# Plain float32 for the first twelve input products, x split after them, and the S5 parameters' complex product on VectorE

## The chip, the cores and the metric

The kernel runs on one core of a Trainium2 chip. The metric is the device time of one execution in microseconds (us), as the median of several runs. The engines are named as the profile names them: PE is TensorE (PEld its weight loads), DVE is VectorE, ACT is ScalarE, POOL is GpSimd and SP is SyncE, which here only issues DMAs. Each engine works through its instructions in an order that a scheduler fixed when the kernel was built; engines wait for one another by semaphores.

## The reference

One layer of an encoder over 512 tokens of width 1024, in float32:

```
xn   = rmsnorm(x, mix_norm_w)
proj = xn @ w_in            # 1024 -> 512 + 1024 + 1536 + 32 + 1024 + 1024
u_s5, z, xbc, dt_raw, gate_a, gate_b = split(proj)
y_a  = s5_bidirectional(u_s5, ...)         # 32 groups, 64 complex states, scan both ways
glu  = gelu(y_a) @ w_glu;  y_a = glu[:1024] * sigmoid(glu[1024:])
y_b  = ssd_bidirectional(z, xbc, dt_raw, ...)   # convolution over 5 tokens, chunked scan, w_ssd_out
h    = x + (sigmoid(gate_a) * y_a + sigmoid(gate_b) * y_b) @ w_o
h    = h + peer_ffn(rmsnorm(h, ffn_norm_w), ...)  # 16384 experts, 8 heads, 16 picks of each
out  = rmsnorm(h, final_norm_w)
```

The S5 part needs, for every group, products of two complex factors that come from the parameters alone (powers of lambda times the discretised B).

## The kernel before, in words

**Stages.** The first 560 us or so of the execution are the front part: the norm of x, the products with `w_in`, S5, SSD and the gated linear unit. Then come the merge with `w_o`, the routing and the two forms of the expert layer (dense and gathered), to 1963 us.

**Split products.** Every large product is done with its two operands split: `hi` is the operand rounded to float32r by ACT, `lo` is what is left, made by a subtraction on DVE or POOL. `mm3` (lines 147 to 153) then issues three products for each block of 128 inner elements: hi times hi (L151), hi times lo (L152), lo times hi (L153).

**The stream of jobs.** `stream_T` runs over a list of jobs. A job is one weight tile [128, 8, 128] of `w_in` times x in its transposed form ([128, 8, 512]); its output is [128, 512]. `wload` (L136 to L145) brings the tile of the next job while the present one runs: a DMA that SP issues into `w_raw` (three buffers, L140), a cast by ACT into `w_hi` (L143), a subtraction into `w_lo` (L144) on the engine that a table of zeros and ones names (0 DVE, 1 POOL). Then come 24 products into the tile `mm` and an evacuation by ACT. The jobs come in the order u 0 to 3, gate_b 0 to 3, the convolution's B and C tiles 8 to 11, dt (32 columns wide), the convolution's x tiles 0 to 7, and the rest. Of the first twelve jobs the tables give six `w_lo` to DVE and six to POOL.

**x.** `norm_T` (L189 to L199) transposes x with TensorE into the tile `sm`, and for each of 8 blocks ACT writes `xh` (L197) and DVE writes `xl` (L198).

**S5 beside the stream.** `weave` traces the first 22 jobs (`N_IN`) side by side with S5, which has eight parameter groups q. For each q, `s5_params` (L315 on) makes the factors `mpr`, `mpi` by a complex product, `cmul` (L244 to L250), of six operations over 128x512 on POOL:

```
mr, mi, gt = big("mpr"), big("mpi"), big("s5tmpg")
self.cmul(mr, mi, pw(self.pm[0]), pw(self.pm[1]), ch(bbr), ch(bbi), gt, eng=G)
```

and `x0r`, `x0n` by six operations over 128x512 on DVE (L338 to L344). TensorE takes `mpr` and `mpi` by transposes (L374). `s5_data` does the chunk products (L434 to L436) into `sm`. The convolution of a tile takes four operations on DVE (L464) and one at its end (L466). The rest of the list of jobs is woven with SSD.

**Tiles.** `xh` and `xl` are two tiles of [128, 8, 512] under the tags Ah and Al; in the merge `mh` and `ml` take the same places. `col`, a row of 0 to 127, is made by POOL at the start and used by the routing.

Of the kernel before, what the change touches and what calls it, by code (L numbers as in the profile page):

```python
# [10 lines left out]
F32 = mybir.dt.float32  # L11
# [15 lines left out]
P_GLU = (1,)  # L27
# [12 lines left out]
N_IN = 22  # L40
LAST = 2
# [13 lines left out]
# columns of the array of small parameters  # L55
# [9 lines left out]
def weave(*fibers):  # L65
    """Runs (generator, length) pairs side by side, each at its own pace."""
    live = [[g, 0, float(n)] for g, n in fibers]
    while live:
        live.sort(key=lambda f: f[1] / f[2])
        f = live[0]  # L70
        try:
            next(f[0])
            f[1] += 1
        except StopIteration:
            live.remove(f)


def ahead(tc, gen, offset):
    """The steps of gen, traced at a higher priority."""
# [9 lines left out]
class Kernel:  # L89
# [8 lines left out]
    # ---------------------------------------------------------------- constants  # L98
    def consts(self):
# [4 lines left out]
        # half the taps and biases: silu(x) = (tanh(x / 2) + 1) x / 2  # L104
# [4 lines left out]
        col = cp.tile([128, 128], F32, name="col")  # L109
        nc.gpsimd.iota(col, pattern=[[1, 128]], base=0, channel_multiplier=0,  # L110
                       allow_small_or_imprecise_dtypes=True)
# [3 lines left out]
        self.col = col  # L115
# [14 lines left out]

    def pc(self, name, i=None):
        a, b = PAR[name]
        return self.par[:, a:b] if i is None else self.par[:, a + i:a + i + 1]

    # ---------------------------------------------------------------- products
    def wload(self, src, k, m, name="w", lo_eng=None):  # L136
        """A weight tile [128, k, m] as its two float32r parts."""
# [9 lines left out]
    def mm3(self, ps, ahi, alo, bhi, blo, nk, start=True, stop=True):  # L147
        """ps += a^T b, each operand as (high, low); k runs over nk blocks."""
# [10 lines left out]
    def stream_T(self, jobs):  # L159
        """Products with the weight tiles of jobs = [(src, k, m, xh, xl, evacuate, lo_eng)], outputs [m, 512]."""  # L160
        load = lambda j: self.wload(j[0], j[1], j[2], lo_eng=self.nc.gpsimd if j[6] else self.nc.vector)
        nxt = load(jobs[0])
        for i, (src, k, m, xh, xl, evac, _) in enumerate(jobs):
            hi, lo = nxt
            if i + 1 < len(jobs):
                nxt = load(jobs[i + 1])
            ps = self.pmm.tile([128, 512], F32, name="mm", tag="mm", bufs=2)
            self.mm3(ps[:m], lambda q: hi[:, q, :], lambda q: lo[:, q, :],
                     lambda q: xh[:, q, :], lambda q: xl[:, q, :], k)
# [3 lines left out]
    def jobs(self, srcs, k, xh, xl, pool):  # L173
        """One job for each (src, m, evacuate)."""
        return [(src, k, m, xh, xl, ev, pool[i % len(pool)]) for i, (src, m, ev) in enumerate(srcs)]

    # ---------------------------------------------------------------- norm to T-layout
    def rstd(self, src, name, t):
        """1 / rms of the rows of tile t."""
# [9 lines left out]
    def norm_T(self, xr, wname, hi, lo):  # L189
        """xr: 4 tiles [128 t, 1024], scaled by their rstd; hi, lo: [128, 8, 512]."""  # L190
        nc = self.nc
        for d in range(8):
            ps = self.psm.tile([128, 512], F32, name="sm", tag="sm", bufs=4)
            for t in range(4):
                nc.tensor.transpose(ps[:, t * 128:(t + 1) * 128], xr[t][:, d * 128:(d + 1) * 128], self.ident)
            w = self.pc(wname, d)
            nc.scalar.activation(hi[:, d, :], ps, AF.Copy, scale=w)  # L197
            nc.vector.scalar_tensor_tensor(lo[:, d, :], ps, w, hi[:, d, :].bitcast(F32),  # L198
                                           op0=OP.mult, op1=OP.subtract)  # L199

    # ---------------------------------------------------------------- S5
    def s5_prep(self):
# [50 lines left out]
        # powers 0..8 of lambda, by k  # L253
# [10 lines left out]
        # by direction: pn[t] = lambda^t | lambda^(7-t), pm[t] = lambda^(8-t) | lambda^(t+1)  # L264
# [13 lines left out]
        # the phase of lambda^8 and its squares, the size of lambda^8  # L278
# [6 lines left out]
        # the phase of lambda^(8 j) over the chunks j  # L285
# [29 lines left out]
    def s5_params(self, q):  # L315
        """What the parameters alone give for groups 4 q to 4 q + 3."""
# [18 lines left out]
        mr, mi, gt = big("mpr"), big("mpi"), big("s5tmpg")  # L335
        self.cmul(mr, mi, pw(self.pm[0]), pw(self.pm[1]), ch(bbr), ch(bbi), gt, eng=G)
# [11 lines left out]
        # lags of the convolution within a chunk  # L348
# [102 lines left out]
    # ---------------------------------------------------------------- SSD  # L451
    def conv(self, f, ps):
        """xbc tile f (0..7 x, 8, 9 B, 10, 11 C) from its projection."""
# [14 lines left out]
    def dt_path(self, ps):  # L468
        """dt and all that hangs on it, from its projection [32, 512]."""
# [56 lines left out]
    def ssd_prep(self):  # L526
        """x and B with the tokens on the partitions, C on both halves."""
# [22 lines left out]
    def ssd_group(self, g):  # L550
# [15 lines left out]
        # the states at the chunks' borders  # L566
# [26 lines left out]
        # C B^T of each chunk, masked for each direction  # L593
# [54 lines left out]
        # + D x, gate, norm over the group's features  # L648
# [30 lines left out]
    # ---------------------------------------------------------------- whole  # L679
    def front(self):  # L680
# [4 lines left out]
        xh = self.big.tile([128, 8, 512], F32R, name="xh", tag="Ah")  # L685
        xl = self.big.tile([128, 8, 512], F32R, name="xl", tag="Al")
# [9 lines left out]
        with tc.tile_pool(name="xp", bufs=4) as xp:  # L696
# [7 lines left out]
            self.norm_T(xt, "mixw", xh, xl)  # L704
        self.dbg("xh", xh.rearrange("p a b -> p (a b)").bitcast(F32))
# [16 lines left out]
        def ev_gb(f):  # L722
            def g(ps):
# [13 lines left out]
        gate_a = self.jobs([(win[24 + f], 128, self.ev_ga(f)) for f in range(8)], 8, xh, xl, P_REST)  # L737
        glu = self.jobs([(I["w_glu"][f], 128, e(f % 8)) for e, a in ((self.ev_gu, 0), (self.ev_gs, 8))
                         for f in range(a, a + 8)], 4, self.yah, self.yal, P_GLU)
        easy = gate_b + rest  # L740
        work = jobs[:4] + easy[:EASY] + jobs[4:] + easy[EASY:]
        for f in range(8):
            work += [gate_a[f], glu[8 + f], glu[f]]
        stream = self.stream_T(work)
# [544 lines left out]
```

## Time and profile before

| | us |
|---|---|
| median of three runs | 1963.23 |
| lowest and highest | 1961.51, 1969.58 |
| span of the profiled execution | 1962.9 |
| PE busy in it | 1817.9 (93%) |
| DVE busy | 1498.9 (76%) |
| ACT busy | 836.4 (43%) |
| POOL busy | 774.4 (39%) |

The profiled execution's span is within 0.4 us of the median, so what is read from it can be set against the median directly. The shares are means over stages of different kinds: the page's 40 slices (49 us each) show PE at six to eight tenths busy in the first five and at nine tenths in nearly all from the twelfth slice on. The change lies in the first 290 us.

### The profile page before, as it was taken

Reading aid. Unit: us, or ns where it says so; the run is one execution under the profiler, and the core shown is the slowest. Engines: PE = TensorE matmul, PEld = TensorE weight load, DVE = VectorE, ACT = ScalarE, POOL = GpSimd, SP = SyncE. Lnnn points to the kernel's source line nnn. Section 1 sums busy time; section 2 is a strip of 40 time slices with the busy share of each in tenths; the row PEclk is TensorE's granted clock in tenths of the full one; section 3 lists DMA queues with packets and bytes.
Section 4 is the critical chain, followed back from the end, with each engine's and each line's share of the span. In section 5 each row is a group of like instructions: output and inputs, shape, how many; then the busy total and the mean of one; then the engine's idle time right before and its main releaser. Section 6 shows DMA issues by size and latency. Waiting matters only on the chain.

```text
span 1962.9 us, 27293 instructions
## 1 busy us (share of the span) xinstructions
PE 1817.9 (93%) x9447; PEld 1580.4 (81%) x9447; DVE 1498.9 (76%) x3238; ACT 836.4 (43%) x1426; POOL 774.4 (39%) x637
## 2 busy tenths in 40 slices
PE   6778889999998987887899999999999999999998
PEld 4666667767887877877898999999999999999886
DVE  7999875677645789998867977777777777777676
ACT  4333545455332333967762333333333333333333
POOL 3364403444112345554543543343434343343341
PEclk9889899999999998998999999999999999999999
DMA  4212153454552223424379998889899889886665
GB/s 141 91 44 82 54 139 125 157 155 141 199 180 79 98 80 129 183 108 183 119 250 334 363 334 294 305 309 313 278 314 313 301 283 313 306 284 230 234 259 200
DMA packets 174826, 407.45 MB, mean 208 GB/s; under 512 B 20000, under 2 KB 77088, under 8 KB 171616
## 3 DMA queue, kind: packets, MB, share of 16 engines
q1 hardware_dynamic: 129472, 258.27, 39.0%
q0 software_dynamic: 36864, 134.23, 19.3%
q10 hardware_dynamic: 8352, 13.21, 1.9%
q8 instruction: 74, 1.21, 0.3%
q14 instruction: 64, 0.52, 0.1%
HBM read 367.28 MB, written 37.32 MB: 206 GB/s over the span
## 4 chain that ended last, share of the span: by engine, by line
PE 59%; DVE 10%; ACT 2%; DMA 2%; issue 1%; POOL 1%; DVEq 0%; POOLq 0%; ACTq 0%
PE acc L1075 9%; PE acc L1076 9%; PE acc L1074 8%; PE hid L153 7%; PE hid L151 7%; PE hid L152 7%; PE mm L151 3%; PE mm L153 3%; PE mm L152 3%; PE sm L1020 2%; DVE oh L1001 2%; DMA G<-G_d 2%; DVE oh L1002 1%; DVE ohm L935 1%; ACT stg L1021 1%
## 5 line engine op out<-in xcount | busy, mean ns | idle before, releaser
L143 ACT CAST w_hi<-w_raw 128x1024 fp32r<-128x1024 f32 (+2 forms) x209 | 211.8, 1014 | 459.7 <-PE hid L152 220.4
L153 PE MATMUL hid<-x2h,w_lo 128*128 128x384 f32 x1024 | 357.3, 349 | 12.8 <-POOL w_lo L144 9.2
L151 PE MATMUL hid<-x2h,w_hi 128*128 128x384 f32 x1024 | 355.5, 347 | 9.7 <-ACT w_hi L143 9.7
L144 POOL TENSOR_TENSOR w_lo<-w_raw,w_hi 128x1024 fp32r<-128x1024 f32 (+1 forms) x94 | 218.6, 2327 | 361.5 <-ACT w_hi L143 354.7
L152 PE MATMUL hid<-x2l,w_hi 128*128 128x384 f32 x1024 | 355.0, 347 | 0.0
L1091 POOL DMA_INDIRECT rowg<-in_u_dram,idx x128 | 191.8, 1498 | 276.8 <-DVE rowg L1103 191.9
L1076 PE MATMUL acc<-vh,Wl 128*128 128x512 f32 x768 | 300.7, 392 | 0.0
L1075 PE MATMUL acc<-vl,Wh 128*128 128x512 f32 x768 | 300.6, 391 | 0.0
L1074 PE MATMUL acc<-vh,Wh 128*128 128x512 f32 x768 | 298.5, 389 | 0.0
L1091 POOL DMA_INDIRECT rowg<-in_v_dram,idx x128 | 167.6, 1310 | 272.2 <-DVE acc L1113 209.1
L144 DVE TENSOR_TENSOR w_lo<-w_raw,w_hi 128x1024 fp32r<-128x1024 f32 (+1 forms) x115 | 140.9, 1225 | 169.1 <-ACT w_hi L143 169.1
L153 PEld LDWEIGHTS hid<-x2h,w_lo 128*128 128x128 f32 x1024 | 197.6, 193 | 14.8 <-POOL w_lo L144 11.0
L151 PEld LDWEIGHTS hid<-x2h,w_hi 128*128 128x128 f32 x1024 | 197.4, 193 | 14.2 <-ACT w_hi L143 10.5
L156 ACT CAST Wh<-F 128x384 fp32r<-128x384 f32 x128 | 65.9, 515 | 317.8 <-PE acc L1075 279.7
L152 PEld LDWEIGHTS hid<-x2l,w_hi 128*128 128x128 f32 x1024 | 197.3, 193 | 3.7
L1076 PEld LDWEIGHTS acc<-vh,Wl 128*128 128x128 f32 x768 | 144.1, 188 | 30.3
L157 DVE TENSOR_TENSOR vl<-v_raw,vh 128x1024 fp32r<-128x1024 f32 x128 | 156.2, 1220 | 14.2 <-ACT vh L156 13.3
L1075 PEld LDWEIGHTS acc<-vl,Wh 128*128 128x128 f32 x768 | 144.1, 188 | 28.5 <-DVE vl L157 0.2
L1074 PEld LDWEIGHTS acc<-vh,Wh 128*128 128x128 f32 x768 | 144.2, 188 | 28.3 <-ACT vh L156 0.4
L1113 DVE SCALAR_TENSOR_TENSOR acc<-rowg,act,acc 128x1024 f32<-128x1024 f32 x127 | 162.4, 1279 | 5.9 <-DMA rowg<-in_v_dram,idx 5.7
L1103 DVE SCALAR_TENSOR_TENSOR rowg<-rowg,xn 128x1024 f32<-128x1024 f32 x128 | 152.0, 1219 | 5.1 <-DMA rowg<-in_u_dram,idx 5.1
L153 PE MATMUL mm<-xh,w_lo 128*128 128x512 f32 (+1 forms) x328 | 136.8, 418 | 15.9 <-DVE w_lo L144 12.3
(392 smaller groups left out, 3553.1 us busy)
## 6 DMA issues: line engine op xcount, KB each, us to landing
w_raw<-in_ut_dram SPq DMA_DIRECT2D x128, 512.0 KB, 4.7
v_raw<-in_v_dram SPq DMA_DIRECT2D x128, 512.0 KB, 6.5
G_d<-stg SPq DMA_DIRECT2D x24, 1024.0 KB, 3.9
G<-G_d SPq DMA_DIRECT2D x16, 1536.0 KB, 13.8
w_raw<-in_w_in_dram SPq DMA_DIRECT2D x40, 512.0 KB, 3.6
RB<-rows_d SPq DMA_DIRECT2D x32, 256.0 KB, 5.6
w_raw<-in_w_q_dram SPq DMA_DIRECT2D x16, 512.0 KB, 3.5
E<-rows_d SPq DMA_DIRECT2D x32, 128.0 KB, 5.0
```

The costliest lines, as they stand in the source:

```text
L143: nc.scalar.copy(hi, raw)
L144: (lo_eng or nc.vector).tensor_sub(lo, raw, hi.bitcast(F32))
L151: mm(ps, ahi(k), bhi(k), start=start and k == 0, stop=False)
L152: mm(ps, ahi(k), blo(k), start=False, stop=False)
L153: mm(ps, alo(k), bhi(k), start=False, stop=stop and k == nk - 1)
L157: (lo_eng or self.nc.vector).tensor_sub(lo, src, hi.bitcast(F32))
L1074: mm(a, wh[:, ts], vh[:, hs], start=k == 0, stop=False)
L1075: mm(a, wh[:, ts], vl[:, hs], start=False, stop=False)
L1076: mm(a, wl[:, ts], vh[:, hs], start=False, stop=k == 127)
L1091: nc.gpsimd.indirect_dma_start(out=r, out_offset=None, in_=tab, in_offset=bass.IndirectOffsetOnAxis(ap=self.idx0[:, k:k + 1], axis=0))
L1103: d = V.scalar_tensor_tensor(r, r, 1.0, self.xn0, op0=OP.mult, op1=OP.mult, accum_out=hid[:, k:k + 1])
L1113: d = V.scalar_tensor_tensor(self.acc0, r, act[:, k:k + 1], self.acc0, op0=OP.mult, op1=OP.add)
```

## The change

The first twelve jobs (u 0 to 3, gate_b 0 to 3, the convolution's tiles 8 to 11) no longer use split operands: each of the 8 blocks is one product of `w_raw` with x in plain float32 (L176 of the kernel after). These jobs have no cast and no subtraction of weights. `norm_T` writes x unsplit into eight tiles of [128, 512] of a ring of nine, and `xl` is not written there. The split of x comes in the evacuation of the twelfth job (`parts`): 8 casts by ACT and 8 subtractions by DVE, each of the latter into the ring. `cmul` of `s5_params` goes from POOL to DVE and shares the temporary tile `s5tmp` with the operations of `x0r`. `mh` of the merge lies in the ring, and `col` is made before the routing. Comments are dropped, so line numbers shift.

```diff
+N_RAW = 12
@@ consts
-        col = cp.tile([128, 128], F32, name="col")
-        nc.gpsimd.iota(col, ...)
+    def ring(self, dt):
+        return self.big.tile([128, 512], dt, name="ring", tag="ring", bufs=9)
@@ stream_T
-        load = lambda j: self.wload(j[0], j[1], j[2], lo_eng=self.nc.gpsimd if j[6] else self.nc.vector)
+        def load(j):
+            if j[4] is None:
+                raw = self.wp.tile([128, j[1], j[2]], F32, name="w_raw", tag="w_raw", bufs=3)
+                self.nc.sync.dma_start(raw, j[0])
+                return raw, None
+            return self.wload(j[0], j[1], j[2], lo_eng=self.nc.gpsimd if j[6] else self.nc.vector)
...
-            self.mm3(ps[:m], lambda q: hi[:, q, :], lambda q: lo[:, q, :],
-                     lambda q: xh[:, q, :], lambda q: xl[:, q, :], k)
+            if lo is None:
+                for q in range(k):
+                    self.nc.tensor.matmul(ps[:m], hi[:, q, :], xh[q], start=q == 0, stop=q == k - 1)
+            else:
+                self.mm3(ps[:m], lambda q: hi[:, q, :], lambda q: lo[:, q, :],
+                         lambda q: xh[:, q, :], lambda q: xl[q], k)
@@ norm_T
-            nc.scalar.activation(hi[:, d, :], ps, AF.Copy, scale=w)
-            nc.vector.scalar_tensor_tensor(lo[:, d, :], ps, w, hi[:, d, :].bitcast(F32),
-                                           op0=OP.mult, op1=OP.subtract)
+            nc.scalar.activation(raw[d], ps, AF.Copy, scale=self.pc(wname, d))
@@ s5_params
-        mr, mi, gt = big("mpr"), big("mpi"), big("s5tmpg")
-        self.cmul(mr, mi, pw(self.pm[0]), pw(self.pm[1]), ch(bbr), ch(bbi), gt, eng=G)
+        mr, mi, gt = big("mpr"), big("mpi"), tmp
+        self.cmul(mr, mi, pw(self.pm[0]), pw(self.pm[1]), ch(bbr), ch(bbi), gt)
@@ front
-        xh = self.big.tile([128, 8, 512], F32R, name="xh", tag="Ah")
-        xl = self.big.tile([128, 8, 512], F32R, name="xl", tag="Al")
+        xr = [self.ring(F32) for _ in range(8)]
+        xh = self.big.tile([128, 8, 512], F32R, name="xh", tag="Al")
+        xl = []
...
+        def parts(ev):
+            def f(ps):
+                ev(ps)
+                for d in range(8):
+                    nc.scalar.copy(xh[:, d, :], xr[d])
+                    xl.append(self.ring(F32R))
+                    nc.vector.tensor_sub(xl[d], xr[d], xh[:, d, :].bitcast(F32))
+            return f
+
+        for i in range(N_RAW):
+            src, k, m, _, _, ev, eng = work[i]
+            work[i] = (src, k, m, xr, None, parts(ev) if i == N_RAW - 1 else ev, eng)
@@ merge
-            mh = self.big.tile([128, 8, 512], F32R, name="mh", tag="Ah")
+            mh = [self.ring(F32R) for _ in range(8)]
```

TensorE at the start of its program, before (`sm` is the tile of the transposes of x, `ident` the unit matrix, `mm` the output of a job):

```order
L195 MATMUL sm<-ident,xt 128x128 x32
L151 MATMUL mm<-xh,w_hi 128x512
L152 MATMUL mm<-xl,w_hi 128x512
L153 MATMUL mm<-xh,w_lo 128x512
L151 MATMUL mm<-xh,w_hi 128x512
```

and after (`ring` is a tile of unsplit x; L361 is the first product of S5's parameters):

```order
L205 MATMUL sm<-ident,xt 128x128 x20
L176 MATMUL mm<-ring,w_raw 128x512
L205 MATMUL sm<-ident,xt 128x128 x12
L176 MATMUL mm<-ring,w_raw 128x512 x39
L361 MATMUL sm<-x0r,bm 32x128
```

The three products of a block are now one, and 40 of the 96 (five jobs) stand ahead of the first product of S5.

VectorE in the first parameter group of S5, before (`ur`, `ui` and `d` belong to a chain of small complex squares, `bbr` and `bbi` to the discretised B, `x0r` to the group's factors):

```order
L338 TENSOR_TENSOR x0r<-pnr,s5bc 128x512
L249 TENSOR_TENSOR d_302<-ui,ur 128x32
L245 TENSOR_TENSOR ur<-ur 128x32
L250 TENSOR_TENSOR bbi<-bbi,s5t_579 128x64
L250 TENSOR_TENSOR ui<-ui,d_302 128x32
L339 TENSOR_TENSOR s5tmp<-pni,s5bc 128x512
L246 TENSOR_TENSOR d_302<-ui 128x32
```

and after:

```order
L257 TENSOR_TENSOR bbi<-bbi,s5t_492 128x64
L257 TENSOR_TENSOR ui<-ui,d_275 128x32
L252 TENSOR_TENSOR mpr<-pmr,bbr 128x512
L253 TENSOR_TENSOR d_275<-ui 128x32
L255 TENSOR_TENSOR ui<-ur,ui 128x32
L253 TENSOR_TENSOR s5tmp<-pmi,bbi 128x512
L254 TENSOR_TENSOR ur<-ur,d_275 128x32
L255 TENSOR_TENSOR mpi<-pmr,bbi 128x512
```

The operations of `mpr` and `mpi` now stand in VectorE's row between the small ones.

VectorE at the start, before, where x is split:

```order
L198 SCALAR_TENSOR_TENSOR xl<-sm,par,xh 128x512 x6
L144 TENSOR_TENSOR w_lo<-w_raw,w_hi 128x1024
L198 SCALAR_TENSOR_TENSOR xl<-sm,par,xh 128x512 x2
```

and after, near the middle of the S5 part (L760 is the subtraction of `parts`, L471 the convolution's):

```order
L431 TENSOR_TENSOR spimv<-sc_1156,sc_1157 64x4x63
L760 TENSOR_TENSOR ring<-ring,xh 128x512
L252 TENSOR_TENSOR bbr<-fr,s5bc 128x64
L760 TENSOR_TENSOR ring<-ring,xh 128x512
L254 TENSOR_TENSOR bbr<-bbr,s5t_1477 128x64
L760 TENSOR_TENSOR ring<-ring,xh 128x512
L255 TENSOR_TENSOR bbi<-fr,s5bc 128x64
L760 TENSOR_TENSOR ring<-ring,xh 128x512
L471 SCALAR_TENSOR_TENSOR cvacc<-cvraw,cvw,cvacc 128x512
```

Seven of the eight subtractions of x stand here, after the last plain job; the first, for which the ring has its ninth tile free, stands near the program's start.

## Rows read from the trace of the kernel before

**Rows 1.** Windows: us, busy (x instructions) by engine, granted clock, DMA share, GB/s

```profile
14.00:160.00 146.00, 115.62 (x643) 91.49 (x642) 138.56 (x313) 50.82 (x92) 64.67 (x70) 0.89 0.24 75
160.00:290.00 130.00, 109.25 (x611) 85.04 (x612) 112.56 (x184) 58.82 (x102) 45.72 (x54) 0.91 0.30 84
290.00:560.00 270.00, 256.94 (x1329) 200.96 (x1329) 179.10 (x309) 135.41 (x308) 90.14 (x52) 0.97 0.50 160
```

**Rows 2.** Windows, instructions of tile sm alone (PE, PEld, DVE, ACT)

```profile
14.00:160.00 146.00, 41.56 (x355) 36.10 (x354) 6.27 (x9) 18.90 (x33) 0.89 0.24 75
```

**Rows 3.** Waits of PE, 18 to 290 us: total us, times, longest

```profile
PE sm L435 <- DVE sprev L424: 14.7, 5, 6.2
PE mm L153 <- DVE w_lo L144: 12.3, 3, 8.8
```

**Rows 4.** Waits of SP's queue, 0 to 300 us

```profile
SPq L140 <- DVE w_lo L144: 53.7, 6, 17.1
```

**Rows 5.** DVE's groups, 18 to 290 us: busy us, mean ns, idle before

```profile
L464 DVE SCALAR_TENSOR_TENSOR cvacc<-cvraw,cvw,cvacc 128x512 f32<-128x512 f32 x48 | 42.6, 890 | 0.4
L339 DVE TENSOR_TENSOR s5tmp<-pni,s5bc 128x512 f32<-128x512 f32 x8 | 9.2, 1149 | 0.0
L404 DVE TENSOR_TENSOR scw<-tabc,sin 128x256 f32<-128x256 f32 x8 | 7.4, 920 | 5.5 <-ACT sin L399 5.5
```

**Rows 6.** POOL's groups, 14 to 160 us

```profile
L144 POOL TENSOR_TENSOR w_lo<-w_raw,w_hi 128x1024 fp32r<-128x1024 f32 x6 | 14.9, 2479 | 12.7 <-ACT w_hi L143 12.7
L247 POOL TENSOR_TENSOR mpr<-mpr,s5tmpg 128x512 f32<-128x512 f32 x5 | 8.0, 1601 | 0.0
```

**Rows 7.** DVE's timeline: start us, duration us, instruction

```profile
29.52 2.40 DVE L249 TENSOR_TENSOR etmp<-ei,er 128x32 f32<-128x32 f32 x1
...
43.14 1.13 DVE L246 TENSOR_TENSOR d<-ui 128x32 f32<-128x32 f32 x1
...
45.26 0.68 DVE L340 TENSOR_TENSOR x0r<-x0r,s5tmp 128x512 f32<-128x512 f32 x1
45.86 1.28 DVE L247 TENSOR_TENSOR ur<-ur,d 128x32 f32<-128x32 f32 x1
...
52.92 1.21 DVE L144 TENSOR_TENSOR w_lo<-w_raw,w_hi 128x1024 fp32r<-128x1024 f32 x1
```

**Rows 8.** POOL's timeline of the same stretch

```profile
29.49 2.39 POOL L144 TENSOR_TENSOR w_lo<-w_raw,w_hi 128x1024 fp32r<-128x1024 f32 x1 [2.75 <-ACT w_hi L143]
...
42.59 1.63 POOL L246 TENSOR_TENSOR s5tmpg<-pmi,bbi 128x512 f32<-128x512 f32 x1 [2.77 <-DVE bbi L250]
```

**Rows 9.** PE's timeline at the start and near 95 us (x2: two records)

```profile
15.21 3.68 PE L195 MATMUL sm<-ident,xt 128*128 128x128 f32 x16 [0.92 <-DVE xl L198]
...
92.77 0.38 PE L435 MATMUL sm<-x0r,sprev 128*64 128x128 f32 x2
92.98 0.38 PE L436 MATMUL sm<-x0n,spimv 128*64 128x128 f32 x2
...
95.19 0.40 PE L151 MATMUL mm<-xh,w_hi 128*128 128x512 f32 x1
95.42 0.40 PE L152 MATMUL mm<-xl,w_hi 128*128 128x512 f32 x1
```

**Rows 10.** PE's timeline in a stretch of lower clock

```profile
58.62 0.63 PE L151 MATMUL mm<-xh,w_hi 128*128 128x512 f32 x1
59.05 0.63 PE L152 MATMUL mm<-xl,w_hi 128*128 128x512 f32 x1
```

**Rows 11.** PE's timeline, plain float32 products of one column

```profile
358.41 1.62 PE L664 MATMUL sm<-ones,sq 128*128 128x1 f32 x14
```

**Rows 12.** ACT's timeline, evacuation of the twelfth job

```profile
160.01 0.59 ACT L459 COPY cvraw<-mm 128x512 f32<-128x512 f32 x1 [1.38 <-PE mm L153]
```

**Rows 13.** ACT's groups, 14 to 160 us

```profile
L143 ACT CAST w_hi<-w_raw 128x1024 fp32r<-128x1024 f32 x12 | 12.6, 1047 | 23.7 <-PE mm L152 16.2 <-DVE tabt L249 7.2 <-ACT cs L224 0.2
```

**Rows 14.** DMA issues of the page: KB each, us to landing

```profile
w_raw<-in_w_in_dram SPq DMA_DIRECT2D x40, 512.0 KB, 3.6
```

More of the change, by code (lines that the diff above doesn't have):

```diff
@@ L108, in consts @@
         nc.vector.tensor_scalar(self.nwh, self.pc("ssdnw"), 0.5, None, op0=OP.mult)
-        col = cp.tile([128, 128], F32, name="col")
-        nc.gpsimd.iota(col, pattern=[[1, 128]], base=0, channel_multiplier=0,
-                       allow_small_or_imprecise_dtypes=True)
         rel = self.wp.tile([128, 128], F32, name="rel", tag="w_raw", bufs=3)
@@ L114, in consts @@
                        allow_small_or_imprecise_dtypes=True)
-        self.col = col
         self.ident = cp.tile([128, 128], F32, name="ident")
@@ L187, in rstd, with norm_T @@
         return rs
-    def norm_T(self, xr, wname, hi, lo):
+    def norm_T(self, xr, wname, raw):
         nc = self.nc
@@ L195, in norm_T @@
                 nc.tensor.transpose(ps[:, t * 128:(t + 1) * 128], xr[t][:, d * 128:(d + 1) * 128], self.ident)
-            w = self.pc(wname, d)
-            nc.scalar.activation(hi[:, d, :], ps, AF.Copy, scale=w)
-            nc.vector.scalar_tensor_tensor(lo[:, d, :], ps, w, hi[:, d, :].bitcast(F32),
-                                           op0=OP.mult, op1=OP.subtract)
+            nc.scalar.activation(raw[d], ps, AF.Copy, scale=self.pc(wname, d))
     def s5_prep(self):
@@ L703, in front @@
                 nc.vector.tensor_scalar(xt[t], xt[t], self.rstd(xt[t], "mix", t), None, op0=OP.mult)
-            self.norm_T(xt, "mixw", xh, xl)
-        self.dbg("xh", xh.rearrange("p a b -> p (a b)").bitcast(F32))
+            self.norm_T(xt, "mixw", xr)
         def ev_u(q):
@@ L737, in front @@
         gate_a = self.jobs([(win[24 + f], 128, self.ev_ga(f)) for f in range(8)], 8, xh, xl, P_REST)
+        sl = lambda x: [x[:, q, :] for q in range(x.shape[1])]
         glu = self.jobs([(I["w_glu"][f], 128, e(f % 8)) for e, a in ((self.ev_gu, 0), (self.ev_gs, 8))
-                         for f in range(a, a + 8)], 4, self.yah, self.yal, P_GLU)
+                         for f in range(a, a + 8)], 4, self.yah, sl(self.yal), P_GLU)
         easy = gate_b + rest
@@ L837, in f @@
                     V.scalar_tensor_tensor(mr[:, i, :], mr[:, i, :], 0.5, g, op0=OP.mult, op1=OP.add)
-                    A.activation(mh[:, i, :], mr[:, i, :], AF.Copy, scale=0.5)
-                    V.scalar_tensor_tensor(ml[:, i, :], mr[:, i, :], 0.5, mh[:, i, :].bitcast(F32),
+                    A.activation(mh[i], mr[:, i, :], AF.Copy, scale=0.5)
+                    V.scalar_tensor_tensor(ml[:, i, :], mr[:, i, :], 0.5, mh[i].bitcast(F32),
                                            op0=OP.mult, op1=OP.subtract)
                 return f
-            for _ in self.stream_T(self.jobs([(I["w_so"][i], 128, ev_y(i)) for i in range(8)], 8, yh, yl, P_SO)):
+            for _ in self.stream_T(self.jobs([(I["w_so"][i], 128, ev_y(i)) for i in range(8)], 8, yh, [yl[:, q, :] for q in range(8)], P_SO)):
                 pass
@@ L859, in merge @@
                     ps = self.pmm.tile([128, 512], F32, name="mm", tag="mm", bufs=2)
-                    self.mm3(ps, lambda q: mh[:, q, ts], lambda q: ml[:, q, ts],
+                    self.mm3(ps, lambda q: mh[q][:, ts], lambda q: ml[:, q, ts],
                              lambda q: wo[q // 2][0][:, q % 2, :], lambda q: wo[q // 2][1][:, q % 2, :], 8)
@@ L888, in ev @@
             return f
-        for _ in self.stream_T(self.jobs([(I["w_q"][i], 128, ev(i)) for i in range(16)], 8, self.x2h, self.x2l, P_Q)):
+        for _ in self.stream_T(self.jobs([(I["w_q"][i], 128, ev(i)) for i in range(16)], 8, self.x2h, [self.x2l[:, q, :] for q in range(8)], P_Q)):
             yield
@@ L1187, in whole @@
                 self.kT = {}
+                self.col = self.hp.tile([128, 128], F32, name="col")
+                nc.gpsimd.iota(self.col, pattern=[[1, 128]], base=0, channel_multiplier=0,
+                               allow_small_or_imprecise_dtypes=True)
                 self.first = self.rp.tile([128, 16, 8], BF16, name="first")
```

## The prediction

> **What bounds the kernel now.** I read four views in this order: the page's 40 slices, the windows over the stages that the change touches, the waits, and the groups and timelines of the engines that wait.
>
> The windows [rows 1] give the busy time of PE, PEld, DVE, ACT and POOL in that order. From 14 to 160 us (the first twelve jobs) DVE is busy 138.6 of 146 us, idle 7.4, while PE is busy 115.6. From 160 to 290 us (the ten jobs that still run beside S5) DVE has 112.6 and PE 109.3 of 130. From 290 to 560 us PE has 256.9 of 270. So the first stretch is bound by DVE, the second by DVE and PE in turn, and the third by PE. PE's longest waits before 290 us say the same: 14.7 us for `sprev` and 12.3 us for `w_lo`, both made by DVE [rows 3]. The last product of the twelfth job is evacuated at 160.0 us [rows 12]; what comes sooner there is the gain, as long as the later stretches keep their lengths.
>
> DVE's 138.6 us are partly not its own. Two operations of 512 columns that run undisturbed start 0.60 us apart with a duration of 0.68 (45.26 and 45.86) [rows 7], yet the eight of L339 have a mean of 1.149, the eight 128x256 ones of L404 0.920, and the 48 of L464 0.890 [rows 5]. The timelines show why. A 128x32 operation lasts 2.40 us from 29.52, to 31.92, while POOL subtracts a weight from 29.49 to 31.88. Another lasts 1.13 from 43.14, to 44.27, while POOL's L246 runs to 44.22 [rows 7, 8]. A DVE operation that meets POOL there ends when POOL's ends.
>
> For every DVE operation from 18 to 290 us I took its duration less the lower quartile of its own form, and put the excess to the POOL operation that ran beside it. The excess is 62.4 us: 40.4 beside the 48 operations of `cmul` (24.6 before 160 us, where five groups lie, 15.8 after) and 21.3 beside POOL's twelve `w_lo` (10.6 before, 10.7 after). That is about 0.84 us for a `cmul` operation and 1.8 for a `w_lo`, of the 1.60 and 2.48 that they last [rows 6].
>
> The Trainium skill, page "SBUF — State Buffer", section "Who interferes with whom", has VectorE and GpSimd share a pair of ports by an exclusive lock, and lets a VectorE operation with two SBUF inputs contend with GpSimd's reads. If the lock took all of POOL's time, the excess would be POOL's full durations; the trace has about half of that for `cmul`.
>
> **The change, part by part: 14 to 160 us, DVE.** Start from 138.6. The `cmul` excess goes: −24.6. The six POOL `w_lo` of the first twelve jobs go with theirs: −10.6. Six `w_lo` on DVE go: duration 1.21 [rows 7], 0.08 less as a pitch (as 0.68 against 0.60), so 6 × 1.13 = −6.8. The eight writes of `xl` at the start go, as STT of 512 columns at about 0.66: −5.3. What comes: 30 of `cmul`'s operations at the pitch of L340, 30 × 0.60 = +18.0, and the first subtraction of x, +0.6. The sum is 109.9; with the idle 7.4 kept, 117.3, so DVE would be through at 14 + 117 = 131 us. Bounds: if the excess moved elsewhere instead of leaving, DVE would have 138.6 − 6.8 − 5.3 + 18.6 = 145; if all POOL time were DVE's (64.7 of [rows 1]), 138.6 − 64.7 + 6.5 = 80, and PE would decide.
>
> **14 to 160 us, PE.** A split product of 512 columns starts 0.23 us after the one before (95.19, 95.42), and a plain float32 product of 128 columns shows as two records in 0.22 us (92.77 to 92.98) [rows 9]. No plain product of 512 columns is in this trace. Four times 0.217 gives 0.87, against 3 × 0.23 = 0.69 for the three that it replaces. So a job goes from 5.5 to 7.0 us and twelve take 96 × 0.87 = 83.5. From below, a plain product can't be cheaper than two split ones, 0.46, unless the two records of the 128-column product are mostly fixed cost; from above, see the first two rivals. I take 0.87, since the nearest row is a plain float32 product. PE's work on `sm` in the window is 41.6 us [rows 2], of which 3.7 are transposes of x before the first product [rows 9]: 38 stay. The first plain product needs neither a cast nor a subtraction and can start near 16 us instead of 18.9. So PE, never idle, would be through at 16 + 83.5 + 38 = 138 us.
>
> PE at 138 and DVE at 131, each waiting now and then for the other, give 140 for the twelfth evacuation, 20 us sooner than 160. The 2 us over PE's sum are my choice; before, the bounding engine's own idle time was 7.4.
>
> **160 to 290 us.** On DVE: −15.8, + 18 × 0.60 = +10.8 for three groups of `cmul`, + 7 × 0.60 = +4.2 for the other subtractions of x. That is −0.8. Six `w_lo` stay on POOL with their excess of 10.7. The first split job needs a cast, a subtraction and all of `xl` at once: seven subtractions stand in one piece of DVE's row just before it. It costs PE a gap of 1 to 2 us if nothing of S5 fills it. Together 0 to +1 us.
>
> **After 290 us.** 256.9 of 270 us are PE's, with the same products as before, so an earlier start is passed on whole, and the rest of the program has the same order from the merge's `w_o` products on.
>
> **What costs nothing, and what covers it.** ACT loses 12 casts of 1.05 [rows 13] and gets 8 of 512 columns; it is busy 50.8 of 146, so even if all 8 casts of x came in a row while PE waited, it would be some 5 us. SP: a plain job's weight load waits until PE is through with the job three before (three buffers), where now it waited 53.7 us for DVE's `w_lo` [rows 4]. It is then two jobs (14 us) ahead, against 3.6 us to landing [rows 14]; behind it on SP's queue stand the loads of `U` and `toe`, which may wait up to one job, 7 us, and PE's chunk products with them; the twelve jobs give PE other work in that time. If not, it is worth one or two such waits, some 5 us, which the range holds. `s5tmp` now serves `cmul` and `x0r` in turn, both on DVE in order, so it adds no wait. `mh` in the ring and `col` before the routing are one POOL operation and another address: nothing.
>
> **Rivals.**
>
> *Plain products cannot hide their weight loads.* Products of one column come at 1.62/14 = 0.116 us per record [rows 11], as long as 128 columns (0.109), so a record seems to pay at least a weight load. If a 512-column product paid two loads on top of its columns, 0.87 + 2 × 0.111 = 1.09, the twelve jobs would take 104.6 and PE be through at 16 + 104.6 + 38 = 159: no gain, 1962. Against it: split products show weight loads beside the product before (PEld busy 91.5 within PE's 115.6 [rows 1]).
> The Trainium skill, page "TensorE: Matmul & The Clock Gate", section "LDWEIGHTS (loading the stationary operand)", gives a load as the column count over 1.2, an estimate of 107 ns for 128 columns, and the section "Weight-path perf modes — Fast Weight Load (FWL) and DoubleRow" sees no win for float32 from fast loads; the row's 0.116 agrees with the first, and the rest no row here shows.
>
> *Slower: the plain products run at the lower clock.* From 58.62 to 59.05 the pitch is 0.43, against 0.23 [rows 9, 10]: the 1.2 GHz level of TensorE, where the window's mean granted clock is 0.89 [rows 1]. If plain products met that level all along, they would take 96 × 1.74 = 167 and PE end at 221, 61 us late: 2024. The place is PE before the twelfth evacuation. Each us of plain work at the lower level costs one more; the 22 us between 138 and 160 are used up at 22/83.5 = 26% of them, and it is slower by over 0.5% from 32/83.5 = 38%. Against it: with PE busier than before in the stretch, there are fewer gaps ahead of which the clock fell.
>
> *PE is not the bound.* If a plain product is as cheap as two split ones, 0.46, PE ends at 16 + 44 + 38 = 98 and DVE decides: 131, perhaps 127 with less idle time. That is 29 to 33 us of gain, 1930 to 1934.
>
> *The change doesn't do what it says.* If DVE's long operations are not POOL's doing, DVE has 145 + 7.4 = 152 in the first stretch and 112.6 + 15 in the second: +6 and +15, or 1984. The matching ends of [rows 7, 8] speak against it.
>
> **How the numbers follow.** 1963 − 20 + 1 = 1944. Chances: this forecast 0.60; weight loads not hidden 0.14; plain products cheap 0.15; lower clock 0.08; POOL not the cause 0.03. About 0.5% (9.8 us) is what a measurement of this kernel can tell from no change. Faster by more: 0.57 of the forecast's 0.60 and the cheap case's 0.15, 0.72. Within it: 0.03, 0.14 and 0.01 of the last two, 0.18. Slower: 0.10. The range goes from 1927 (cheap products, 3 us beyond) to 1964 (weight loads in full), which leaves out the slow cases and the edges of the others.
>
> **What would show it.** In the profile after: the plain product's pitch in PE's timeline, 0.87 (or 1.09, 0.46, 1.74); the twelfth job's evacuation near 140; DVE's 512-column operations at 0.68 instead of 0.9 to 1.15 where POOL has no `w_lo`; DVE busy near 110 us up to the twelfth job; the stretch between the twelfth job and the last convolution (130 us) and the 270 us after it unchanged. A second stretch that is longer by more than 5 us would say that the split of x or the `cmul` operations on DVE hold up the split jobs, and the sum fails there. So would a PE idle for long in the first stretch, with a wait for `mpr` or `x0r` in place of that for `w_lo`.

## The result, and the profile after

The changed kernel takes 1928.7 us (median of 4 runs, 1924.8 to 1931.5); the kernel before, run with it, 1965.9. The ratio is 0.9828, with a 95% interval of 0.9804 to 0.9853: 29 to 39 us faster. The forecast was 1944, some 19 us faster; the measured time lies in its range, close to the low end. The sign held and so did the mechanism of the first stretch; the gain came out nearly twice as large, and most of what is beyond the forecast lies in the second stretch.

The profiled execution has a span of 1925.9 us, 37.0 less than that of before. Two marks cut it. The evacuation of the twelfth job moved from 160.01 us [rows 12] to 137.39. The last operation of the convolution, the end of the S5 part, moved from 289.85 to 256.36. From ACT's and DVE's timelines, of the kernel after, and the last line of the kernel before:

```profile
137.39 0.59 ACT L466 COPY cvraw<-mm 128x512 f32<-128x512 f32 x1 [1.49 <-DVE ks L367]
...
256.36 0.69 DVE L473 SCALAR_TENSOR_TENSOR xcT<-cvraw,cvacc 128x512 f32<-128x512 f32 x1 [0.31 <-ACT cvraw L472]
```

```profile
289.85 0.69 DVE L466 SCALAR_TENSOR_TENSOR xcT<-cvraw,cvacc 128x512 f32<-128x512 f32 x1
```

| stretch | before | after | moved | forecast |
|---|---|---|---|---|
| start to the twelfth evacuation | 160.0 | 137.4 | −22.6 | −20 |
| from there to the last xcT | 129.9 | 119.0 | −10.9 | 0 to +1 |
| from there to the end of the span | 1673.0 | 1669.5 | −3.5 | 0 |

These are single traces. A second trace of the changed kernel, shown further down, has 140.0, 120.1 and 1671.3, so a stretch is good to one to three us. The last row can't be told from nothing: over all traces of this case, whose edits lie before that mark, the last stretch has 1665.2 to 1677.3.

The windows of the kernel after over the first two stretches (us, busy of PE, PEld, DVE, ACT, POOL, granted clock, DMA share, GB/s), against [rows 1]:

```profile
14.00:137.40 123.40, 120.58 (x551) 68.19 (x549) 109.89 (x323) 44.38 (x90) 14.57 (x35) 1.00 0.29 85
137.40:256.40 119.00, 104.19 (x611) 83.24 (x612) 109.22 (x211) 59.80 (x109) 17.00 (x35) 0.94 0.35 100
```

In the first stretch TensorE is now the bound, busy 120.6 of 123.4 us at a granted clock of 1.00 (2.4 GHz throughout), and DVE's busy time is the forecast 109.9. In the second, DVE is busy 109.2 where before it had 112.6, a small change, but its idle time fell from 17.4 to 9.8. That is where the sum was off.

The plain product is settled by one row of PE's timeline, after:

```profile
18.15 33.64 PE L176 MATMUL mm<-ring,w_raw 128*128 128x512 f32 x78
```

These are 39 products in two records each: 33.64/39 = 0.863 us, four times the 0.217 of the 128-column product in [rows 9]. Weight loads stay hidden (PEld busy 68 beside PE's 121). This rules out the rivals that had 1.09, 0.46 or the lower clock's 1.74.

The groups of DVE, 14 to 256.4 us, that answer to [rows 5], and POOL's largest:

```profile
L471 DVE SCALAR_TENSOR_TENSOR cvacc<-cvraw,cvw,cvacc 128x512 f32<-128x512 f32 x48 | 40.0, 836 | 0.4
L346 DVE TENSOR_TENSOR s5tmp<-pni,s5bc 128x512 f32<-128x512 f32 x8 | 5.4, 681 | 0.0
L411 DVE TENSOR_TENSOR scw<-tabc,sin 128x256 f32<-128x256 f32 x8 | 3.4, 420 | 2.7 <-ACT sin L406 2.7
```

```profile
L144 POOL TENSOR_TENSOR w_lo<-w_raw,w_hi 128x1024 fp32r<-128x1024 f32 x6 | 15.8, 2634 | 17.7 <-ACT w_hi L143 17.7
```

The eight operations of L346 (L339 before) have a mean of 681 ns instead of 1149, those of L411 (L404) 420 instead of 920. Taken by the prediction's method, DVE's excess is 2.7 us before the twelfth evacuation (35.8 before the change) and 10.2 after it (26.7), of which 9.9 beside five of the six weight subtractions that POOL has left (the first of the six begins at 130.75 us, in the first stretch).

### The profile page after: what moved, and what is told of

It is laid out like the page before. It is cut to its first block, busy times and chain, and to the rows that moved or that the text cites. A ratio compares the mean times of both kernels' runs of the same rounds, so it can differ in the third digit from the quotient of the medians.

```text
span 1925.9 us, 27091 instructions
## 1 busy us (share of the span) xinstructions
PE 1815.1 (94%) x9351; PEld 1553.0 (81%) x9351; DVE 1466.3 (76%) x3280; ACT 828.4 (43%) x1422; POOL 697.7 (36%) x583
## 4 chain that ended last, share of the span: by engine, by line
PE 60%; DVE 11%; DMA 3%; ACT 2%; issue 1%; POOL 1%; DVEq 0%; POOLq 0%; SPq 0%; ACTq 0%
PE acc L1097 9%; PE acc L1098 9%; PE acc L1096 9%; PE hid L153 7%; PE hid L151 7%; PE hid L152 7%; PE mm L151 3%; PE mm L153 3%; PE mm L152 3%; PE sm L1042 3%; DMA G<-G_d 2%; DVE oh L1023 2%; DVE oh L1024 1%; DVE ohm L957 1%; PE sm L903 1%
## 5 line engine op out<-in xcount | busy, mean ns | idle before, releaser
L143 ACT CAST w_hi<-w_raw 128x1024 fp32r<-128x1024 f32 (+2 forms) x197 | 199.2, 1012 | 446.6 <-PE hid L152 213.3
L144 POOL TENSOR_TENSOR w_lo<-w_raw,w_hi 128x1024 fp32r<-128x1024 f32 (+1 forms) x88 | 204.0, 2320 | 364.2 <-ACT w_hi L143 361.4
L144 DVE TENSOR_TENSOR w_lo<-w_raw,w_hi 128x1024 fp32r<-128x1024 f32 (+1 forms) x109 | 132.7, 1217 | 173.2 <-ACT w_hi L143 173.2
L1042 PE MATMUL sm<-oh,oh 128*128 128x128 f32 x768 | 131.8, 298 | 12.2 <-DVE oh L1024 12.1
```

Source lines behind the costliest of these rows:

```text
L143: nc.scalar.copy(hi, raw)
L144: (lo_eng or nc.vector).tensor_sub(lo, raw, hi.bitcast(F32))
L1042: T.matmul(ps[:, j * 128:(j + 1) * 128], o2, o1, start=True, stop=True)
```

## The experiments

Two readings of the second stretch stood open. Theory A: it became shorter because `cmul` no longer stretches DVE's operations there. Theory B: S5 gets ahead of the jobs in the first stretch, where TensorE is the bound now, and has less left. A third, theory L, says that POOL's `cmul` cost time as a slow link in the chain of dependences, and not by what it does to DVE.

**One part alone: plain products, `cmul` on POOL.** The changed kernel with

```diff
-        mr, mi, gt = big("mpr"), big("mpi"), tmp
-        self.cmul(mr, mi, pw(self.pm[0]), pw(self.pm[1]), ch(bbr), ch(bbi), gt)
+        mr, mi, gt = big("mpr"), big("mpi"), big("s5tmpg")
+        self.cmul(mr, mi, pw(self.pm[0]), pw(self.pm[1]), ch(bbr), ch(bbi), gt, eng=G)
```

> The changed kernel with cmul of s5_params back on GpSimd (own temporary tile): only the plain products and the later split of x remain. The changed kernel's profile has the twelfth evacuation at 137.4 us and 119.0 us from there to the last xcT at 256.4, where the kernel before had 160.0 and 129.9. Theory A (the second stretch became shorter because cmul's GpSimd time no longer stretches VectorE's operations, and with them the waits between TensorE, ScalarE and VectorE): first stretch to 140-146 us (VectorE 138.6 - 10.6 - 6.8 - 5.3 + 0.6 = 116.5 busy and 7.4 idle, TensorE 138), second stretch 130 to 134 (as before, plus 4.2 for the split of x), so 1945 to 1953 in all. Theory B (the second stretch became shorter because the plain products make the first one TensorE's, so that S5 gets ahead by about 5 us or more and has less left after the twelfth job): second stretch 119 to 125, so 1934 to 1940.

Measured: 1957.2 us, ratio 0.9959 (0.9942 to 0.9977), 5 to 11 us faster than before: less than either theory gave. Its windows, and from the first stretch PE's longest wait:

```profile
14.00:155.40 141.40, 125.60 (x574) 72.44 (x572) 122.94 (x303) 44.88 (x94) 51.80 (x66) 0.96 0.29 79
155.40:283.60 128.20, 107.85 (x595) 85.67 (x595) 110.18 (x180) 56.91 (x99) 42.27 (x53) 0.89 0.31 85
```

```profile
PE sm L401 <- ACT mT L382: 10.7, 1, 10.7
```

The second stretch (128.2) was as long as before, which speaks for A. The first was off, 155.4 instead of 140 to 146: neither engine is full there. Part of it is one wait of PE, and three timelines of this kernel show how a late DVE reaches PE through a queue (DVE, then ACT with its DMA issues):

```profile
62.74 1.75 DVE L254 TENSOR_TENSOR tabc<-tabc,tabt 128x512 f32<-128x512 f32 x1
...
69.22 0.20 DVE L367 TENSOR_TENSOR ks<-ks,dg 16x64 f32<-16x64 f32 x1
```

```profile
69.46 0.33 ACTq L369 DMA_DIRECT2D kd<-ks  x1
69.83 0.44 ACTq L371 DMA_DIRECT2D kd<-ks  x1
70.31 0.58 ACT L382 COPY mT<-sm 128x512 f32<-128x512 f32 x1 [13.30 <-DVE tabt L256]
```

ACT's queue issues the DMA of `ks`, whose last addition is DVE's at 69.22, behind 128x512 operations of the tables of which several lasted 1.6 to 1.75 us beside POOL's `cmul`. The copy `mT` that PE needs stands behind that DMA. Its tile was ready long before.

**The other part alone: `cmul` on DVE, all products split.** The kernel before with the same two lines turned round (`tmp` and no `eng=G`).

> The kernel before with one edit: cmul of s5_params on VectorE with the shared temporary tile; all products stay split. Theory A: first stretch 138.6 - 24.6 + 18.0 = 132 busy and 7 idle, so the twelfth evacuation near 153; second stretch shorter by 5 (-15.8 + 10.8) to 11 us, since the contention of cmul is gone; in all 12 to 18 us faster than before. Theory B: second stretch within 2 us of 129.9, in all about 7 us faster.

Measured: 1944.5 us, ratio 0.9896 (0.9868 to 0.9923), 15 to 26 us faster, 20 by the ratio, a little over what theory A gave and far from B's 7. Its windows:

```profile
14.00:140.50 126.50, 108.80 (x611) 86.78 (x610) 121.11 (x322) 50.71 (x90) 29.70 (x41) 0.96 0.29 85
140.50:269.80 129.30, 107.82 (x643) 85.45 (x644) 115.94 (x224) 60.16 (x109) 21.21 (x36) 0.92 0.32 87
```

The cut at the twelfth job misled me here: the twelfth evacuation came 19.5 us sooner, not 7, and the second stretch was no shorter. The order of jobs against S5 is another one (643 PE instructions lie in the second stretch, against 611), so that work of S5 slid behind the mark: four parameter groups have their `cmul` before it, where the kernel before has five. Over both stretches, to the last xcT at 269.8, it gains 20.1 us. The first part alone gains 6.3 to that mark, both together 33.5 (29.7 in the second trace): more than the sum, by 3 to 7 us. The totals show this less clearly. By the ratios, 0.9959 × 0.9896 = 0.9855, with some 0.003 to either side, against 0.9828, and 0.9794 in the later set. That each part is worth more beside the other is likely, and not shown.

**The late groups back to POOL.** The changed kernel with `cmul` on POOL where `q >= 5`, the three groups after the twelfth job:

```diff
+        if q >= 5:
+            self.cmul(mr, mi, pw(self.pm[0]), pw(self.pm[1]), ch(bbr), ch(bbi), gt, eng=G)
+        else:
+            self.cmul(mr, mi, pw(self.pm[0]), pw(self.pm[1]), ch(bbr), ch(bbi), tmp)
```

> The changed kernel with cmul on GpSimd for the last three parameter groups alone (q = 5, 6, 7), which lie after the twelfth job; the first five stay on VectorE. Theory A: first stretch as in the changed kernel (137), second stretch back to 127-132 us, in all 8 to 13 us slower than the changed kernel (1936 to 1941). Theory B: second stretch 119 to 122, within 3 us of the changed kernel.

**The early groups back to POOL.** The same with `q < 5`.

> The changed kernel with cmul on GpSimd for the first five parameter groups (q = 0 to 4), the last three on VectorE. VectorE in the first stretch: 109.9 - 18.0 + 24.6 = 116.5, below TensorE's 120.6 of 123.4. Theory A: first stretch to 138-143, second stretch 117-121, in all 1 to 6 us slower than the changed kernel. Theory B: S5 loses its lead, second stretch 124-130, in all 6 to 12 us slower.

Measured: 1936.9 us, ratio 0.9863 (0.9835 to 0.9890), for the late groups on POOL; 1943.0 us, 0.9903 (0.9873 to 0.9933), for the early ones. The first lies in theory A's 1936 to 1941. The second stretch of the two, the late ones first:

```profile
136.60:263.00 126.40, 107.25 (x615) 83.39 (x616) 115.31 (x193) 57.52 (x102) 41.94 (x53) 0.93 0.33 92
```

```profile
155.40:274.10 118.70, 102.06 (x584) 81.11 (x585) 105.01 (x198) 58.64 (x103) 17.34 (x31) 0.93 0.34 94
```

With the late groups on POOL the second stretch is 126.4; with them on DVE it is 118.7, although the first stretch is 155.4 and TensorE isn't its bound. Theory A had 127 to 132 and 117 to 121, so its first figure is just missed. Theory B, which wanted 119 to 122 and 124 to 130, falls. Where the `cmul` of the last three groups runs is worth 126.4 − 119.0 = 7.4 us of the second stretch (6.3 against the second trace of the changed kernel), or 128.2 − 118.7 = 9.5 between the two kernels with the early groups on POOL. This price includes whatever the order of instructions does, which differs on DVE, ACT and PE between these kernels. The whole of the early kernel, some 14 us slower than the changed one, was outside A's 1 to 6: its first stretch is that of the first experiment, with the same wait of 10.7 us.

**Stretching without the dependence.** The changed kernel, and beside it in each parameter group six POOL operations of the same form into a tile that nobody reads:

```diff
+        dum = big("s5dum")
+        self.cmul(dum, dum, pw(self.pm[0]), pw(self.pm[1]), ch(c_r), ch(c_i), dum, eng=G)
```

> The changed kernel plus, in each parameter group, six GpSimd operations over 128x512 like those of cmul, on s5bc and the power tables, into a tile that nobody reads. The orders of TensorE, VectorE, ScalarE and SyncE are those of the changed kernel, row by row. Theory C (what GpSimd's cmul cost was the stretching of VectorE's operations): VectorE gets 20 to 25 us of excess back before the twelfth evacuation and about 16 after, and the whole is 15 to 35 us slower than the changed kernel (1944 to 1964). Theory L (what it cost was its own slowness as a link of the chain from the discretised B over mpr and mpi, their transposes and the chunk products, which here runs on VectorE still): the excess shows, but the whole is within 6 us of the changed kernel (1927 to 1935).

Measured: 1972.0 us, ratio to the kernel before 1.0031 (1.0015 to 1.0047). That is 2.0% above the changed kernel's ratio, some 40 us, and more than the whole gain. It is also more than theory C's 1944 to 1964. Nothing reads what these operations write, and the orders of PE, DVE and ACT are those of the changed kernel, instruction by instruction, so theory L falls. The windows, from a trace of this kernel's slowest execution (1978.0 us), and two of the six POOL groups:

```profile
14.00:175.70 161.70, 131.94 (x550) 74.83 (x548) 145.94 (x322) 44.00 (x90) 71.71 (x77) 0.89 0.24 69
175.70:300.50 124.80, 105.79 (x611) 84.78 (x612) 114.09 (x211) 60.03 (x109) 24.93 (x41) 0.92 0.33 90
```

```profile
L252 POOL TENSOR_TENSOR s5dum<-pmr,s5bc 128x512 f32<-128x512 f32 x8 | 14.9, 1858 | 54.6 <-DMA s5bc<-in_s5bc_dram 46.5 <-DVE pmr L279 8.0
L257 POOL TENSOR_TENSOR s5dum<-s5dum 128x512 f32<-128x512 f32 x8 | 9.4, 1179 | 0.6
```

DVE's busy time in the first stretch grew from 109.9 to 145.9, and the stretch by 38.3, from 137.4 to 175.7. By the prediction's method the excess beside the 48 operations is 41.3 us (36.0 and 5.3), 0.86 us for each, as in the kernel before (0.84). Theory C had 20 to 25 and about 16; the first figure is larger because seven of the eight groups of dummy operations fall into the first stretch. DVE's idle time there grew by 2.3 us only, from 13.5 to 15.8, so the longer stretch is DVE's busy time: 36.0 of excess for 38.3. In the second stretch one group of dummy operations is left, and the 124.8 is 4.7 to 5.8 us above the two traces of the changed kernel, for 5.3 of excess. The dummy operations also hold up POOL's small operations behind them: weight loads wait 10.8 us for those, against 1.5 in the changed kernel. The products themselves wait in the first stretch for DVE alone, but for 1.2 us for ACT. TensorE's granted clock fell from 1.00 to 0.89 in the first stretch while its busy share fell from 98% to 82%.

**POOL operations that only write.** The same place, with twelve memsets of 128x512 in each group instead:

```diff
+        dum = big("s5dum")
+        for _ in range(12):
+            G.memset(dum, 0.0)
```

> The changed kernel plus, in each parameter group, twelve GpSimd memsets over 128x512 into a tile that nobody reads; TensorE, VectorE, ScalarE and SyncE have the changed kernel's order. A GpSimd operation that only writes: the Trainium skill, page 'SBUF — State Buffer', section 'Who interferes with whom', says that it does not contend with a VectorE operation of two inputs in SBUF. If so, no excess on VectorE beside the memsets and the whole within 4 us of the changed kernel (1925 to 1933). If any GpSimd operation stretches VectorE as cmul did (half of its time), 96 memsets of 0.5 to 1 us cost VectorE 25 to 50 us, and the whole is 10 to 40 us slower.

Measured: 1936.2 us, ratio 0.9850 (0.9817 to 0.9882), a little above the 1925 to 1933 expected, but not to be told from the changed kernel's 0.9828. POOL's group of this kernel, a window in which POOL does almost nothing but write, two DVE operations in it, and the whole first stretch:

```profile
L346 POOL MEMSET s5dum<- 128x512 f32 x96 | 51.8, 540 | 5.1
```

```profile
25.00:50.00 25.00, 25.00 (x59) 11.02 (x58) 23.26 (x125) 7.99 (x16) 22.62 (x45) 1.00 0.39 120
```

```profile
38.94 0.68 DVE L253 TENSOR_TENSOR s5tmp<-pmi,bbi 128x512 f32<-128x512 f32 x1
39.65 0.68 DVE L255 TENSOR_TENSOR mpi<-pmr,bbi 128x512 f32<-128x512 f32 x1
```

```profile
14.00:144.10 130.10, 124.64 (x552) 70.91 (x552) 114.46 (x331) 44.62 (x89) 62.33 (x126) 0.97 0.28 81
```

POOL is busy 22.6 of these 25 us and DVE's operations keep their 0.68; in the whole of both stretches the excess beside 51.8 us of memsets is under 1 us (0.7 by the prediction's method). So what stretches DVE is not that POOL is busy; of the two kinds tried, those that read SBUF did it and those that only write did not. The Trainium skill, page "SBUF — State Buffer", section "Who interferes with whom", says just that: a VectorE operation with two SBUF inputs contends with a GpSimd operation that reads SBUF, and not with one that only writes. Both halves are borne out here. The memsets cost something otherwise: the twelfth evacuation came at 144.1, 6.7 us later than in the first trace of the changed kernel and 4.1 later than in the second. Of that, the first products came 1.7 us later (17.15 against 15.43), because small POOL operations of the norm queue behind them; PE was busy 4.0 us longer, at a granted clock of 0.97 instead of 1.00. What set that off was not traced.

**The split of x left out.** Seven of eight subtractions gone from the second stretch:

```diff
-                    xl.append(self.ring(F32R))
-                    nc.vector.tensor_sub(xl[d], xr[d], xh[:, d, :].bitcast(F32))
+                    if d == 0:
+                        xl.append(self.ring(F32R))
+                        nc.vector.tensor_sub(xl[d], xr[d], xh[:, d, :].bitcast(F32))
+                    else:
+                        xl.append(xl[0])
```

> The changed kernel without seven of the eight subtractions that split x after the twelfth job: all blocks take the low part of the first (that part of the computation is left out). If the split of x costs VectorE's path its busy time there, 7 x 0.60 = 4.2 us, and the first split job waits for it: the second stretch 113 to 115 instead of 119.0, in all 4 to 6 us faster than the changed kernel. If it lies in time that VectorE has to spare: within 2 us.

**The changed kernel beside it**, on the same chip.

> The changed kernel itself, to stand beside the other three on the same chip: a ratio to the kernel before of 0.980 to 0.985.

Measured: 0.9815 (0.9784 to 0.9846) without the seven, 0.9794 (0.9767 to 0.9822) for the changed kernel itself: no gain. The second stretch without them, and both stretches in the second trace of the changed kernel (its slowest execution of five, 1933.3 us):

```profile
137.50:256.20 118.70, 104.14 (x608) 82.11 (x609) 105.57 (x202) 59.46 (x107) 17.77 (x35) 0.94 0.35 101
```

```profile
14.00:140.00 126.00, 123.24 (x553) 69.89 (x551) 110.25 (x324) 44.65 (x90) 14.63 (x35) 0.99 0.30 84
140.00:260.10 120.10, 106.13 (x609) 84.45 (x610) 108.88 (x210) 59.39 (x109) 17.05 (x35) 0.93 0.36 99
```

DVE's busy time fell from 109.2 to 105.6, but the stretch stayed at 118.7, where 113 to 115 would have shown a cost. The split of x costs nothing that can be seen where it stands: 0.3 us against the first trace of the changed kernel, 1.4 against the second, where these two differ by 1.1.

**More of the same.** Four runs carried the two ideas further. The six weight subtractions that are left on POOL, five of them in the second stretch, to DVE (`P_IN = (0,)`), on two occasions; sixteen plain jobs (`N_RAW = 16`); and both together.

> The changed kernel with the six weight subtractions of the second stretch that are still on GpSimd (2.5 us each) on VectorE: VectorE gets 6 x 1.13 = 6.8 us and loses the 9.9 us by which they stretch it. Theory C: 2 to 5 us faster than the changed kernel (1924 to 1927). If that stretching lies in VectorE's idle time (9.8 of 119 us there), 2 to 7 us slower.

> The changed kernel with the six weight subtractions of the second stretch on VectorE, which had a ratio of 0.9791 to the kernel before on another occasion, beside the changed kernel on the same chip: 2 to 6 us faster than it if the stretching by GpSimd counts in full (-9.9 + 6.8 and a wait for GpSimd of 2 us less); within 2 us of it if the longer row of VectorE makes the products wait for w_lo instead.

> The changed kernel with sixteen plain jobs instead of twelve (dt and the convolution's first three x tiles too), x split after the sixteenth. TensorE gets 4 x 8 x (0.87 - 0.69) = 5.8 us more; VectorE loses the stretching by three GpSimd weight subtractions, 5 us, and dt's subtraction, 0.4. Theory C (the second stretch is VectorE's, and that stretching counts): 0 to 5 us faster than the changed kernel. Theory that TensorE's own work counts in the second stretch: 3 to 6 us slower.

> The changed kernel with sixteen plain jobs and no weight subtraction on GpSimd before SSD. TensorE gets 5.8 us more, VectorE loses the 9.9 us by which GpSimd's subtractions stretch it and gets 3 x 1.13 = 3.4 for the three that stay. If VectorE bounds the second stretch still, 3 to 8 us faster than the changed kernel; if TensorE does by now, 0 to 4 us faster.

Measured: 0.9791 (0.9746 to 0.9836) and 0.9805 (0.9778 to 0.9832) with the subtractions on DVE, 0.9820 (0.9786 to 0.9854) with sixteen plain jobs, 0.9817 (0.9789 to 0.9845) with both; the changed kernel beside the second and the last had 0.9794. None can be told from it, so none of the gains that were expected is shown in a total. The second stretch with the subtractions on DVE, and then with both edits:

```profile
135.80:251.60 115.80, 102.05 (x609) 79.67 (x610) 105.69 (x216) 59.06 (x105) 4.22 (x30) 0.96 0.36 100
```

```profile
135.10:256.60 121.50, 110.27 (x591) 76.16 (x590) 101.34 (x207) 56.46 (x102) 7.95 (x30) 0.96 0.36 99
```

The first does what was expected of it inside the stretch, −3.2 us with −3.5 on DVE, but that is less than the totals can show; its second trace has 116.1, against the second 120.1 of the changed kernel. The last moves the load to TensorE, 110.3 instead of 104.2, and gives back what it saves on DVE. Sixteen plain jobs alone have a second stretch of 122.9, 3 to 4 us longer, as the theory said by which TensorE's own work counts there.

## Why the prediction came out as it did

**The first stretch was right by its parts.** DVE's sum, 109.9, is the measured busy time, although its idle time was 13.5 instead of 7.4. That it agrees to a tenth is luck: some 2 us of the measured time are excess beside the POOL weight subtraction at 130.75, which the sum put after this stretch. TensorE's sum ended at 138, its last plain product at 136.0, and the evacuation came at 137.4 instead of 140. In the second trace it came at 140.0, so the 2 us that I added by choice are neither borne out nor refuted. The order between the engines came out too: TensorE is the bound there now.

**The second stretch is the step that failed**: "−0.8" and "0 to +1 us" against −10.9 (−9.7 in the second trace). Two of its terms were mis-sized.

- "+ 7 × 0.60 = +4.2" for the split of x, and "a gap of 1 to 2 us" at the first split job, measured nothing to speak of: DVE had room for the subtractions, and the first split job, dt, runs woven with S5's products.
- "−15.8, + 18 × 0.60 = +10.8", −5.0 together, measured −6.3 to −9.5 when the late groups went from one engine to the other. I had set the busy time of DVE equal to the length of the stretch and kept its idle time of 17.4, which fell to 9.8. Which of the two numbers is off stays open. Either a longer DVE operation also adds to waits, since DVE and TensorE wait for each other in turn there. Or, as with the split of x, part of the 10.8 of `cmul` on DVE fell into time that DVE had to spare; for this speaks that in the dummy kernel, which adds excess and no work on DVE, a us of excess moved a stretch by about one us. The kernel before shows a place of the first kind, in timelines of DVE, POOL and PE that I had read only as a total:

```profile
240.28 1.78 DVE L344 TENSOR_TENSOR x0n<-x0n,s5tmp 128x512 f32<-128x512 f32 x1
241.99 1.32 DVE L404 TENSOR_TENSOR scw<-tabc,sin 128x256 f32<-128x256 f32 x1
243.24 1.49 DVE L405 TENSOR_TENSOR sc<-tabs,sin 128x256 f32<-128x256 f32 x1
244.65 2.60 DVE L407 TENSOR_TENSOR scv<-tabc,sin 128x256 f32<-128x256 f32 x1
```

```profile
241.59 1.44 POOL L249 TENSOR_TENSOR s5tmpg<-pmi,bbr 128x512 f32<-128x512 f32 x1
243.11 1.34 POOL L250 TENSOR_TENSOR mpi<-mpi,s5tmpg 128x512 f32<-128x512 f32 x1
244.40 2.57 POOL L144 TENSOR_TENSOR w_lo<-w_raw,w_hi 128x1024 fp32r<-128x1024 f32 x1
```

```profile
252.30 0.69 PE L435 MATMUL sm<-x0r,sprev 128*64 128x128 f32 x2 [4.36 <-DVE sprev L424]
```

The three 128x256 operations take 5.4 us instead of the 1.26 of three at 420 ns, and PE waits 4.36 us for `sprev`, the end of that chain. Two of them run beside `cmul`; the longest, 2.60, runs beside a weight subtraction, which the change leaves on POOL. In the second stretch, PE waits for `sprev` 8.3 us in the kernel before, 7.8 with the late groups on POOL, and 1.3 in the kernel after, in this order below; the longest wait that remains there is for a weight:

```profile
PE sm L435 <- DVE sprev L424: 8.3, 3, 4.4
```

```profile
PE sm L445 <- DVE sprev L434: 7.8, 2, 5.5
```

```profile
PE mm L153 <- DVE w_lo L144: 5.0, 1, 5.0
...
PE sm L442 <- DVE sprev L431: 1.3, 1, 1.3
```

That the stretching at those places is what lengthened the waits is argued from these rows; what the runs show is the price of the late groups as a whole. The `cmul` term makes −6.3 to −9.5 of the −9.7 to −10.9, and the split of x about 0. What remains, up to 4.6 us, was not traced.

**The rivals.** Weight loads, the lower clock and the cheap product all fell to the pitch of 0.863 us. The cheap product's 1930 to 1934 came close to the time, by a mechanism that isn't there. It is this rival alone that drew the range down to 1927; that the measured 1928.7 still lies in it is luck. "The change doesn't do what it says" fell to the dummy operations: they give the stretching back, and with it the gain.

## What to carry to other kernels

An operation of two inputs in SBUF that is moved to POOL is not free for a busy DVE: here each 128x512 one on POOL took 0.84 us from DVE, more than the 0.60 that it costs on DVE itself, so price such a move by DVE's operations that end when POOL's do. Where two engines wait for each other in turn, a term of busy time doesn't tell what it moves: here −5.0 us moved the stretch by −6.3 to −9.5, and the +4.2 of the split of x by nothing that can be seen. Before adding up a stretch, look at the waits that begin behind the lengthened operations. And where a stretch is cut at a mark, check that an edit doesn't slide work across it.

## What the runs showed of the hardware

Plain float32 of 512 columns runs at 0.863 us for a product at the full clock, 1.25 times the three split products of 0.23 that it replaces, with the weight loads hidden; so the plain products cost TensorE more, and what they save here lies on ACT and DVE. I had not expected that POOL's memsets leave DVE alone so completely (under 1 us of excess beside 51.8), while POOL's two-input operations took 0.86 us of DVE for each 1.2 to 1.9 us of their own.
